# Interleaving two float32 arrays on one Trainium2 core: each stored row of 32 KiB moved as two pieces of 16 KiB

## The chip, the cores and the metric

The kernel runs on one core of one Trainium2 chip. The metric is the device time of one execution in microseconds (us). Lower is better. Besides the times there is one profiled execution, whose page and trace are read below.

## The reference

Two float32 arrays of 32 x 256 x 1024 elements (32 MiB each) are woven into one of 32 x 256 x 2048 (64 MiB): even places hold x, odd places hold y.

```python
result = np.zeros((batch, seq, dim * 2), dtype=np.float32)
result[..., 0::2] = x
result[..., 1::2] = y
```

Nothing is calculated. The kernel reads 67.11 MB, writes 67.11 MB, and between the two puts every element in its place in on-chip memory.

## The kernel before

The arrays are taken as flat memory and cut into n = 8 blocks. One block of x (or y) is 128 partitions x 8192 floats: each partition holds one contiguous row of 32 KiB, 4 MiB in all. One block of the output is twice as long, 128 rows of 64 KiB, and is stored in two halves (h = 0 and 1) of 128 x 32 KiB, 4 MiB each. So a full load moves 128 rows of 32 KiB, and so does a full store.

There are two buffers for x (`xt`), two for y (`yt`) and two for the woven output (`ot`), all 128 x 8192 floats. `xt` and `yt` alternate by block, `ot` by half.

Three engines work, each with its own order of instructions, tied by semaphores alone:

- **SP issues all loads** on its DMA queue, in this order: the first x block as two halves of 2 MiB (L42, L43), then y of block 0 (L53), x and y of block 1 (L50, L53) and so on. From block 2 on, x of block k waits until the second x copy of block k-2 is done, and y of block k until the second y copy of it is done (the semaphore `woven`, which counts copies). So the loads of block k are issued when block k-2 has been woven completely, and by then only the loads of block k-1 can still be under way.
- **VectorE (DVE) weaves.** For each block and half it copies 128 x 4096 floats of x to the even places of `ot[h]` (L67) and as many of y to the odd places (L70): 32 copies in all. The copy at L67 waits until x has landed and until the previous store from the same `ot[h]` has landed (`osem[h]`); L70 waits for y.
- **The ACT sequencer issues all stores** on its own DMA queue, one for each half when its two copies are done (L83). The very first store is cut in two: 8 KiB of every row (L77, 1 MiB, semaphore `qsem`) and the other 24 KiB (L81, 3 MiB).

At the end ACT waits for the last store from `ot[0]` and SP for the last from `ot[1]`. After the body is written, two SP loads (L42, L43) are moved ahead of the opening barrier, so that they start at once.

What sets the order around the change is therefore: the load queue (17 DMAs), the store queue (17 DMAs), both feeding the same 16 DMA engines, and the copies between them.

Of the kernel before, what the change touches and what calls it, by code (L numbers as in the profile page):

```python
# [3 lines left out]


def _interleave(nc, x, y, out):
    P = 128
    W = 8192
    H = W // 2  # L10

    total = 1
    for s in x.shape:
        total *= s
    n = total // (P * W)
    assert n * P * W == total

    def rows(ap, names, k):
        flat = ap.rearrange("b s d -> (b s d)")
        return flat[k * names : (k + 1) * names].rearrange("(p w) -> p w", p=P)  # L20

    fp32 = mybir.dt.float32
    xt = [nc.alloc_sbuf_tensor(f"xt{b}", [P, W], fp32).ap() for b in (0, 1)]
    yt = [nc.alloc_sbuf_tensor(f"yt{b}", [P, W], fp32).ap() for b in (0, 1)]
    ot = [nc.alloc_sbuf_tensor(f"ot{b}", [P, W], fp32).ap() for b in (0, 1)]

    xsem = [nc.alloc_semaphore(f"xsem{b}") for b in (0, 1)]
    hsem = nc.alloc_semaphore("hsem")
    qsem = nc.alloc_semaphore("qsem")
    ysem = [nc.alloc_semaphore(f"ysem{b}") for b in (0, 1)]  # L30
    woven = nc.alloc_semaphore("woven")
    osem = [nc.alloc_semaphore(f"osem{b}") for b in (0, 1)]


    cuts = [0, W // 4, W]
    parts = [slice(a, b) for a, b in zip(cuts, cuts[1:])]

    xs = [rows(x, P * W, k) for k in range(n)]
    ys = [rows(y, P * W, k) for k in range(n)]
    os_ = [rows(out, 2 * P * W, k) for k in range(n)]  # L40

    nc.sync.dma_start(out=xt[0][:, :H], in_=xs[0][:, :H]).then_inc(xsem[0], 16)  # L42
    nc.sync.dma_start(out=xt[0][:, H:], in_=xs[0][:, H:]).then_inc(hsem, 16)  # L43

    for k in range(n):
        b = k % 2
        if k >= 2:
            nc.sync.wait_ge(woven, 4 * (k - 2) + 3)
        if k:
            nc.sync.dma_start(out=xt[b], in_=xs[k]).then_inc(xsem[b], 16)  # L50
        if k >= 2:
            nc.sync.wait_ge(woven, 4 * (k - 2) + 4)
        nc.sync.dma_start(out=yt[b], in_=ys[k]).then_inc(ysem[b], 16)  # L53

    for k in range(n):
        b = k % 2
        for h in (0, 1):
            c = slice(h * H, (h + 1) * H)
            if h == 0:
                nc.vector.wait_ge(xsem[b], 16 * (k // 2 + 1))  # L60
            elif k == 0:
                nc.vector.wait_ge(hsem, 16)
            if k:
                nc.vector.wait_ge(osem[h], 16 * k)
            if (k, h) == (1, 0):
                nc.vector.wait_ge(qsem, 16)
            nc.vector.tensor_copy(out=ot[h][:, 0::2], in_=xt[b][:, c]).then_inc(woven, 1)  # L67
            if h == 0:
                nc.vector.wait_ge(ysem[b], 16 * (k // 2 + 1))
            nc.vector.tensor_copy(out=ot[h][:, 1::2], in_=yt[b][:, c]).then_inc(woven, 1)  # L70

    for k in range(n):
        for h in (0, 1):
            nc.scalar.wait_ge(woven, 4 * k + 2 * h + 2)
            if (k, h) == (0, 0):
                for c in parts[:-1]:
                    nc.scalar.dma_start(  # L77
                        out=os_[k][:, c], in_=ot[h][:, c]
                    ).then_inc(qsem, 16)
                c = parts[-1]  # L80
                nc.scalar.dma_start(out=os_[k][:, c], in_=ot[h][:, c]).then_inc(osem[h], 16)  # L81
                continue
            nc.scalar.dma_start(  # L83
                out=os_[k][:, h * W : (h + 1) * W], in_=ot[h]
            ).then_inc(osem[h], 16)

    nc.scalar.wait_ge(osem[0], 16 * n)
    used = sorted(s.num for s in [*xsem, hsem, qsem, *ysem, woven, osem[0]])
    assert used == list(range(used[0], used[-1] + 1)), used
    nc.scalar.sem_clear(range(used[0], used[-1] + 1))  # L90
    nc.sync.nop(nofuse=True).wait_op(osem[1], 16 * n, "sem-ge").then_inc(
        osem[1], -16 * n
    )


def kernel(tc, x, y, out):
    nc = tc.nc
    tc.close()
    tc.compile()

    _interleave(nc, x, y, out)

    blocks = nc.main_func.blocks
    for engine in (mybir.EngineType.SP, mybir.EngineType.SP):
        opening = blocks[0].instructions
        at, moved = next(
            (b, i)
            for b in blocks[1:]
            for i in b.instructions
            if i.engine == engine and i.opcode == "DMACopy"  # L110
        )
        assert not (moved.sync_info and moved.sync_info.on_wait)
        body = at.instructions
        body.remove(moved)
        gate = next(
            n
            for n, i in enumerate(opening)
            if i.engine == engine and i.opcode == "Drain"
        )
        opening.insert(gate, moved)  # L120
        at.instructions = body
        blocks[0].instructions = opening


# [1 line left out]
_INS = ['x', 'y']  # L126
_OUTS = [((32, 256, 2048), 'float32')]


# [23 lines left out]
```

## Time and profile before

| what | value |
|---|---|
| time, median of 3 runs | 314.11 us (314.11 to 314.13) |
| span of the profiled execution | 312.9 us |
| what the median adds to the span | 1.2 us (314.11 - 312.9) |
| VectorE busy | 72.0 us in 32 copies, 23% of the span |
| DMA | 134.22 MB at a mean of 429 GB/s |
| load queue (q1) | 2448 packets, 67.11 MB |
| store queue (q10) | 2448 packets, 67.11 MB |

The profiled execution's time is known by its span, from its first to its last instruction; the median of the runs is 1.2 us longer, for what lies before and after. A packet is one piece of contiguous memory moved by one of the 16 DMA engines, or the 4-byte semaphore update by which an engine tells that its share of a DMA has landed. The share of a queue is the time that its packets took, as a part of the time of 16 engines over the span. Besides the page, the trace holds a record of each packet: its queue, bytes, start and duration.

The packets can be counted from the code. Every DMA of 128 rows gives each of the 16 engines 8 rows. The load queue carries 17 DMAs of 128 rows, so 17 x 128 = 2176 rows and 17 x 16 = 272 semaphore updates: 2448. The store queue has 17 DMAs too, and the same count.

### The profile page before, as it was taken

The numbers are of one execution on the slowest core, as the hardware profiler recorded it, in microseconds if no ns is written. First come the engines' busy times: TensorE is split into PE (matmuls) and PEld (weight loads), VectorE is DVE, ScalarE is ACT, GpSimd is POOL, SyncE is SP. The second block draws the span as 40 slices with busy tenths as digits, with TensorE's granted clock in tenths as the row PEclk, the third lists the DMA queues.
The fourth block names the chain that finished last, engine by engine and source line by source line (L and its number), as shares of the span: only waits on it lengthen the run. The fifth ranks groups of instructions, "written<-read, shape, count | busy, mean of one in ns | idle before, by whom it ended". The sixth has DMA issues, their size and how long they took to land.

```text
span 312.9 us, 114 instructions
## 1 busy us (share of the span) xinstructions
DVE 72.0 (23%) x32; POOL 0.2 (0%) x4
## 2 busy tenths in 40 slices
DVE  0216000501305023050220503205032050415410
POOL 0000000000000000000000000000000000000000
DMA  8999999999999999999999999999999999999998
GB/s 337 467 402 436 436 402 419 452 457 415 427 444 411 461 402 469 402 469 402 469 402 465 406 440 432 423 448 402 469 402 469 402 469 402 469 402 448 423 423 381
DMA packets 4896, 134.22 MB, mean 429 GB/s; under 512 B 544, under 2 KB 544, under 8 KB 544
## 3 DMA queue, kind: packets, MB, share of 16 engines
q1 hardware_dynamic: 2448, 67.11, 50.1%
q10 hardware_dynamic: 2448, 67.11, 49.7%
HBM read 67.11 MB, written 67.11 MB: 429 GB/s over the span
## 4 chain that ended last, share of the span: by engine, by line
DMA 82%; DVE 12%; issue 0%
DMA out_dram<-ot 76%; DMA yt<-in_y_dram 6%; DVE ot L70 6%; DVE ot L67 6%
## 5 line engine op out<-in xcount | busy, mean ns | idle before, releaser
L67 DVE COPY ot<-xt 128x4096 f32<-128x4096 f32 x16 | 36.7, 2295 | 213.8 <-DMA out_dram<-ot 206.5
L70 DVE COPY ot<-yt 128x4096 f32<-128x4096 f32 x16 | 36.6, 2288 | 12.3 <-DMA yt<-in_y_dram 12.3
L137 POOL MEMSET const-bfloat16-1.0<- 128x1 bf16 x1 | 0.1, 103 | 0.0
L137 POOL MEMSET const-uint8-127<- 128x1 uint8 x1 | 0.1, 102 | 0.0
L137 POOL MEMSET const-float32-0.0<- 128x1 f32 x1 | 0.1, 100 | 0.2 <-issue 0.2
L137 POOL MEMSET const-float32-1.0<- 128x1 f32 x1 | 0.1, 99 | 0.0
## 6 DMA issues: line engine op xcount, KB each, us to landing
out_dram<-ot ACTq DMA_DIRECT2D x15, 4096.0 KB, 34.1
yt<-in_y_dram SPq DMA_DIRECT2D x8, 4096.0 KB, 41.5
xt<-in_x_dram SPq DMA_DIRECT2D x7, 4096.0 KB, 24.3
xt<-in_x_dram SPq DMA_DIRECT2D x2, 2048.0 KB, 9.5
out_dram<-ot ACTq DMA_DIRECT2D x1, 3072.0 KB, 32.8
out_dram<-ot ACTq DMA_DIRECT2D x1, 1024.0 KB, 16.3
```

The lines of the kernel that those rows point to most:

```text
L67: nc.vector.tensor_copy(out=ot[h][:, 0::2], in_=xt[b][:, c]).then_inc(woven, 1)
L70: nc.vector.tensor_copy(out=ot[h][:, 1::2], in_=yt[b][:, c]).then_inc(woven, 1)
L137: nc = _bacc.Bacc("TRN2", target_bir_lowering=False, num_devices=1)
```

## The change

Stores name their rows as two pieces. The access pattern of the store, on the on-chip side and on the memory side, goes from (128 rows x 8192 floats) to (128 rows x 2 pieces x 4096 floats); for the second part of the first store from (128 x 6144) to (128 x 2 x 3072). The bytes, their places and the order of the stores stay. The helper writes the instruction itself, with the same queue as before, so that the two pieces stay separate in the pattern. The first part of the first store (8 KiB rows) and all loads are as before. No wait, buffer or copy changes, and no instruction is added on any engine: ACT issues 17 DMAs as before, 16 of them with the new pattern.

```diff
+QUEUES = {
+    mybir.EngineType.SP: "qSPDynamicHW",
+    mybir.EngineType.Activation: "qActDynamicHW",
+}
+
+def _piece_copy(engine, out, in_, s):
+
+    ins, outs = (
+        engine.lower_ap_dma(ap.rearrange("p (s w) -> p s w", s=s)) for ap in (in_, out)
+    )
+    return engine.add_instruction(
+        mybir.InstDMACopy(
+            mode="Copy",
+            name=engine.bass.get_next_instruction_name(),
+            engine=engine.engine,
+            ins=ins,
+            outs=outs,
+            queue=QUEUES[engine.engine],
+        )
+    )
...
                 c = parts[-1]
-                nc.scalar.dma_start(out=os_[k][:, c], in_=ot[h][:, c]).then_inc(osem[h], 16)
+                _piece_copy(nc.scalar, os_[k][:, c], ot[h][:, c], 2).then_inc(osem[h], 16)
                 continue
-            nc.scalar.dma_start(
-                out=os_[k][:, h * W : (h + 1) * W], in_=ot[h]
+            _piece_copy(
+                nc.scalar, os_[k][:, h * W : (h + 1) * W], ot[h], 2
             ).then_inc(osem[h], 16)
```

## The prediction

> **What bounds the kernel now.** I read the page's busy lines first, then its DMA queues, then the chain of work that ended last, then the packet records.
>
> ```profile
> DVE 72.0 (23%) x32; POOL 0.2 (0%) x4
> ...
> DMA  8999999999999999999999999999999999999998
> ...
> q1 hardware_dynamic: 2448, 67.11, 50.1%
> q10 hardware_dynamic: 2448, 67.11, 49.7%
> ```
>
> VectorE works 23% of the span. The 16 DMA engines are full from the second slice to the last but one: the two queues' packets take 50.1 + 49.7 = 99.8% of all engine time. So the DMA engines are the bound, in every stage; a chain that names stores only says which transfer a copy happened to wait for:
>
> ```profile
> 76.83 2.29 DVE ot L67
> 79.12 2.21 DVE ot L70
> 81.34 0.02 issue
> 81.36 34.17 DMA out_dram<-ot
> 115.53 0.02 issue
> 115.55 2.29 DVE ot L67
> 117.85 2.21 DVE ot L70
> 120.06 0.02 issue
> 120.08 34.17 DMA out_dram<-ot
> ```
>
> The columns are start, length and what. The steady round is 115.55 - 76.83 = 38.72 us, in which one block (8 MiB in, 8 MiB out) moves. A store lands 34.17 us after its issue, though its own share of an engine is only 8 rows: it waits behind the store before it and shares the engines with the loads. Bandwidth in stretches says the same:
>
> ```profile
> 13.00:24.00 11.00, 2.09 (x1) 0.00 (x0) 1.00 1.00 432
> ...
> 100.00:260.00 160.00, 36.78 (x17) 0.00 (x0) 1.00 1.00 433
> ```
>
> (The last columns are the DMA share and GB/s.) Loads alone reach 432, loads and stores mixed 433. Nothing is lost by mixing.
>
> **What one packet costs.** The packet records do not name the engine, but a record starts where its predecessor on the same engine ended, so they fall into 16 chains. I take the step from one start to the next. In the steady part 32 KiB rows step by 1209.5 ns (2249 of them, mean), loads or stores alike. The 16 KiB rows of the first two loads step by 607.0 ns. The first store's 8 KiB and 24 KiB rows lie alternately with 32 KiB load rows, in cycles of 1515.4 and 2117.7 ns; less 1209.5 that is 305.9 and 908.2 ns. All four lie on one line: 602.4 ns for 16 KiB plus 4.7 ns a packet. So cutting a 32 KiB row in two costs 2 x 607.0 - 1209.5 = 4.5 ns, or 4.7 by the line; the store rows alone (8 and 24 KiB) give 305.9 - 602.3 / 2 = 4.7.
>
> **Who is served.** The same chains show the order: with both queues waiting, an engine takes one row of one queue, then one of the other, whatever their sizes. Around 100 us one engine starts q10 at 99.244, q1 at 100.453, q10 at 101.663, each 32 KiB; around 35 us it takes an 8 KiB store row (306 ns), a 32 KiB load row (1209), and so on. The small store then got a fifth of the engine. This matters more than the cost of the packet.
>
> **The change part by part.**
>
> *Added packets.* Sixteen stores of 128 rows become 256 pieces each: 16 x 128 = 2048 packets more, 128 on each engine. At 4.7 ns that is 128 x 4.7 = 0.60 us (0.58 by the 4.5). Since the engines have no idle time, nothing hides it. The bytes and the 272 semaphore updates stay.
>
> The Trainium skill, page DMA: Bandwidth & Descriptors, section Why small descriptors are slow (HBM only), gives a fixed overhead of about 3 cycles a packet, and its Specifications a fabric of 850 MHz; an estimate from these is 128 x 3.5 ns = 0.45 us, and the time would be 314.56. The rows here say 4.7 ns, and rows decide.
>
> *Shares.* While loads wait too, an engine now alternates 1209.5 ns of load and 607 ns of store. Stores fall from a half of the engine to a third. Loads of one block (16 rows on each engine) need 16 x (1209.5 + 607) = 29.1 us instead of 38.7. Then SP can issue nothing until the next block is woven, and stores run alone for 16 x 607 = 9.7 us. Together 38.8 us: the same round. I followed both queues, the copies and the waits row by row by these rules; for the kernel before it gives 311.6 us to the last landing, where the chains end at 312.2 to 312.5. For the change no engine is ever without a packet. The closest places: the first 24 KiB store lands near 67 us instead of 57, so the first copy of block 1 starts 10 us later, its store is issued near 72, but the store ahead ends only near 79; and at the end the last store is issued some 4.5 us before the one ahead of it has ended, in both kernels (here 298.1 against 302.6). If that cover were gone, a hole of a copy pair and the start of a store would stand open, 4.5 us and about 1 us (SP's first load: issued at 0.00, first packet at 0.99).
>
> *Issues.* An ACT issue takes 0.34 us (L83); a pattern with twice the pieces could take longer, which I bound by nothing and twice that, 0.34 us. Behind it on ACT stands only the next store's wait, about 14 us off in the steady part, so I take zero.
>
> *Load queue falling idle.* This is new. In the trace before, the load queue never runs dry until 277 us. Now it does once a round, and wakes for blocks 3 to 7: five times. Before shows one such wake beside a busy queue, the first store's: between 25 and 33 us each engine's rows run late by 0.35 to 0.62 us, median 0.46. Loads starting on idle engines lost 0.73 (median, first 5 us). The other neighbour is the ending of the loads at 277 us: rows step 1209 before and after, zero. So one wake costs 0 to 0.73 us, five of them 0 to 3.6. I take zero, nearest to this row: a store row (SBUF to memory) is already in the pipe at each wake, as after 277, while at 25 us the first write of all entered. Memory reads need time to start, but a row that is asked for early hides it: the first store's rows ran some 3.4 us after they could (issue done at 24.62, first row near 28.7, against 0.6 us on an idle engine).
>
> *Sum.* Span 312.86 + 0.60 = 313.46; with the 1.25 us around it 314.71, against 314.11. That is +0.19%, and about 0.2% (0.63 us, to 314.74) is what a measurement of this kernel can tell from no change. The forecast stands on the edge of it.
>
> **Rivals.**
>
> *B, slower: each wake of the load queue costs.* Place: the first load row after stores ran alone, five times. Price: at 0.46 us each 2.3, so 317.0; at 0.73, 318.4; at 0.1, 315.2. It decides from about 0.01 us each, since the packets already stand at the bound. For it: the one wake seen, late on all 16 engines. Against: three later changes of pattern (57 us, 24 to 32 KiB; 277 us; the 16 to 32 KiB loads at 11.5) cost nothing that can be seen.
>
> The same page, section Queues, rings and completion order, has an engine drain a packet of some 9 to 17 descriptors from one ring before it turns; then a whole DMA's share would be one turn, loads and stores would keep their halves, the load queue would not fall idle, B would be out, and the time would be that of the sum. The trace disagrees: it turns after each row.
>
> *C, no change: the pieces are joined again* on the way to the engines (they are contiguous on both sides). Then 314.11. Against it: the built pattern keeps 2 x 4096, and rows of 16 KiB do exist on the load side.
>
> *D, faster: the losses at the start shrink.* Behind 31 us the chains lose only 0.08 us (39 to 43.5 us, median) and nothing after. If the change gave back all of that 0.08 and all of the first store's 0.46, it would still add 0.60 - 0.54 = 0.06 us: 314.17 at best. A gain of over 0.2% would need faster rows, and all four sizes lie on one line.
>
> **How the numbers follow.** Forecast 0.55 (314.6 to 314.9 by 4.5 to 5.1 ns a packet and a possible 0.1 at the start); of it I put 0.32 within the bound and 0.23 above. B 0.30. C 0.07. Something that opens a hole in the store queue 0.05, slower. D or any other gain 0.03. So faster 0.03, same 0.32 + 0.07 = 0.39, slower 0.23 + 0.30 + 0.05 = 0.58. The likeliest single case is still the plain sum, 314.71. Range: from C, 314.1, to 317.4, which takes in B up to 0.53 us a wake, and leaves out about a quarter of B, D, and half of the holes: some 0.13 to 0.15.
>
> **What would show it.** Store queue: 2448 + 2048 = 4496 packets at the same 67.11 MB; 2448 would be C. Loads land sooner: x about 19 us after issue instead of the 24.3 of the page's DMA issues, y about 31 instead of 41.5; stores stay near 34. Unchanged landings with 4496 packets would mean that the shares are not by row. The longest wait of L67 grows from 29.0 to about 38.7 us. The steady round is 38.8 us; 39.3 would be B at 0.46. DMA stays at 9s throughout; an 8 in the middle would be a hole. I am wrong if the time is below 314.1, or if a round stays at 38.8 and the time still rises.

## The result, and the profile after

| | before | after |
|---|---|---|
| time, median | 314.14 us (314.11 to 314.40, 6 runs) | 315.21 us (315.16 to 316.75, 6 runs) |
| span of the profiled execution | 312.9 us | 313.9 us |

The change is 1.07 us slower by the medians: a ratio of 1.004, 95% interval 1.0026 to 1.0053. That lies inside the range and on the side that held most of the chance, but half a microsecond above the sum of 314.71, and above the 314.6 to 314.9 that were given to the sum. One of the six runs took 316.75; the six of the kernel before lie within 0.3 us.

The page of the changed kernel, DMA slices and queues (packets, MB, share of 16 engines):

```profile
DMA  8999999999999999999999999999999999999998
...
DMA packets 6944, 134.22 MB, mean 428 GB/s; under 512 B 544, under 2 KB 544, under 8 KB 544
...
q1 hardware_dynamic: 2448, 67.11, 50.0%
q10 hardware_dynamic: 4496, 67.11, 49.9%
```

The store queue has 4496 packets, as counted, so the pieces stay apart. The engines are as full as before, 99.9%, and no slice shows a hole. What takes longer is therefore in the packets themselves.

The DMA issues of the page before, then of the same page after (KB each, median us from issue to landing):

```profile
out_dram<-ot ACTq DMA_DIRECT2D x15, 4096.0 KB, 34.1
yt<-in_y_dram SPq DMA_DIRECT2D x8, 4096.0 KB, 41.5
xt<-in_x_dram SPq DMA_DIRECT2D x7, 4096.0 KB, 24.3
```

```profile
out_dram<-ot ACTq DMA_DIRECT2D x15, 4096.0 KB, 34.2
yt<-in_y_dram SPq DMA_DIRECT2D x8, 4096.0 KB, 31.7
xt<-in_x_dram SPq DMA_DIRECT2D x7, 4096.0 KB, 18.8
```

Loads land after 18.8 and 31.7 us (about 19 and 31 were forecast; before 24.3 and 41.5), stores as late as before. The engines do alternate packet by packet, and loads have two thirds of the time while both wait. From the changed kernel's chain of waits (start, length, what), one round, and the starts of the later ones:

```profile
85.20 0.02 issue
85.22 34.39 DMA out_dram<-ot
119.61 0.02 issue
119.64 2.29 DVE ot L90
121.93 2.21 DVE ot L93
124.14 0.02 issue
124.17 34.40 DMA out_dram<-ot
...
163.10 0.02 issue
...
201.90 0.02 issue
...
240.71 0.02 issue
...
279.50 0.02 issue
```

This round is 124.14 - 85.20 = 38.94 us where 38.80 was forecast; the later ones are 38.96, 38.80, 38.81 and 38.79. The first two rounds are longer by 0.15 us each, the others are as forecast. The longest wait of the first copy grew from 29.0 to 37.6 us (38.7 forecast), by the views of the waits before and after:

```profile
DVE ot L67 <- DMA out_dram<-ot: 206.5, 14, 29.0
```

```profile
DVE ot L90 <- DMA out_dram<-ot: 207.4, 14, 37.6
```

**The ledger by packet records.** For each of the 16 chains I take every step from one packet's start to the next, less what the line gives (602.4 ns for 16 KiB, plus 4.7 ns). What is left is lateness. Mean of 16 engines, in us, and the start of the last semaphore packet of the middle and of the slowest engine:

| kernel | 0 to 50 us | after 50 us | middle engine ends | slowest ends |
|---|---|---|---|---|
| before | 1.18 | 0.00 | 312.34 | 312.47 |
| after | 1.35 | 0.12 | 313.15 | 313.48 |

The slowest engine ends 1.00 us later. Of that 0.60 are packets, 0.17 the first 50 us, and 0.12 late rows in the rounds (23 rows late by over 20 ns, all of them 32 KiB load rows, near 97, 136 and 174 us). The rest, about 0.1, is the balance of two terms: engines end farther apart (0.33 us from the middle one to the slowest, 0.13 before), and their first packets start 0.07 us earlier in the mean. Each of the three is small, and the experiments ask which of them belongs to the change.

### The profile page after: what moved, and what is told of

It reads as the page before. It is cut to its first block, busy times and chain, and to the rows that moved or that the text cites. A ratio compares the mean times of both kernels' runs of the same rounds, so it can differ in the third digit from the quotient of the medians.

```text
span 313.9 us, 114 instructions
## 1 busy us (share of the span) xinstructions
DVE 72.0 (23%) x32; POOL 0.2 (0%) x4
## 3 DMA queue, kind: packets, MB, share of 16 engines
q1 hardware_dynamic: 2448, 67.11, 50.0%
q10 hardware_dynamic: 4496, 67.11, 49.9%
## 4 chain that ended last, share of the span: by engine, by line
DMA 79%; DVE 12%; another core or an unknown queue 3%; issue 0%; ACTq 0%; DVEq 0%
DMA out_dram<-ot 73%; DVE ot L93 6%; DMA yt<-in_y_dram 6%; DVE ot L90 6%; ACTq L100 0%; DVEq L89 0%
## 5 line engine op out<-in xcount | busy, mean ns | idle before, releaser
L93 DVE COPY ot<-yt 128x4096 f32<-128x4096 f32 x16 | 36.6, 2290 | 12.3 <-DMA yt<-in_y_dram 12.3
## 6 DMA issues: line engine op xcount, KB each, us to landing
yt<-in_y_dram SPq DMA_DIRECT2D x8, 4096.0 KB, 31.7
xt<-in_x_dram SPq DMA_DIRECT2D x7, 4096.0 KB, 18.8
out_dram<-ot ACTq DMA_DIRECT2D x1, 3072.0 KB, 41.5
```

## Experiments

The theory is the sum: 4.7 ns for every packet more, nothing else. Against it stood that each wake of the load queue costs (rival B), that cut stores make the stall at the start longer, and that the helper's instruction itself costs. The kernel before was timed beside each set: 314.23 us (26 runs) beside the first four kernels, 314.22 (9) beside the next four, 314.33 (9) beside the last two.

### one_piece: the helper without the cut

```diff
-                _piece_copy(nc.scalar, os_[k][:, c], ot[h][:, c], 2).then_inc(osem[h], 16)
+                _piece_copy(nc.scalar, os_[k][:, c], ot[h][:, c], 1).then_inc(osem[h], 16)
...
-                nc.scalar, os_[k][:, h * W : (h + 1) * W], ot[h], 2
+                nc.scalar, os_[k][:, h * W : (h + 1) * W], ot[h], 1
```

> The helper writes the stores, but each row stays one piece (128 x 1 x 8192, first store 128 x 1 x 6144): the change without its cut. Theory of the sum (4.7 ns for every packet more, plus a stall when the first stores join): 2448 packets on the store queue, time as before, 314.1 to 314.4; the engines run late by about 0.48 us between 25 and 33.5 us, as before. Rival, the helper itself costs (its instruction differs): 315.2 with 2448 packets.

Measured 314.30 us, ratio 1.0002 (0.9993 to 1.0011), 2448 packets. The helper costs nothing, though an ACT issue takes 0.48 us with it (0.34 before, 0.61 with two pieces): the issue is hidden. Lateness from 0 to 50 us is 1.17, after that 0.00.

### first_block_whole: 14 of 16 stores cut

```diff
+                _piece_copy(nc.scalar, os_[k][:, c], ot[h][:, c], 1).then_inc(osem[h], 16)
...
+                nc.scalar, os_[k][:, h * W : (h + 1) * W], ot[h], 2 if k else 1
```

> The three stores of block 0 keep whole rows, the other 14 are cut in two: 14 x 8 = 112 packets more on each engine. Theory that the part beyond the sum (1.07 us measured, 0.60 of it packets) is the longer issue of cut stores at the start: 0.53 us of packets and no more, 314.65 to 314.8, with 0.48 us late at 25 to 33.5 us. Rival, the stall at the start varies from run to run and has nothing to do with the cut: as the whole change less 0.08, about 315.1. Rival, each wake of the load queue costs: five wakes remain, the excess stays, about 315.1, and rows run late at the five wakes.

Measured 315.03 us, ratio 1.0038 (1.0023 to 1.0052); three of the nine runs took 315.51 to 317.14. The stall between 25 and 33.5 us is 0.50, 0.48 before, and still the time is 0.80 above, not 0.53. So here the start is not where the excess comes from. The load queue falls idle four times in this kernel, not the five that were expected: with whole stores in block 0 it does not run dry before block 3. Three engines have late rows (0.10, 0.19 and 0.38 us in the rounds); the engine with 0.38 is the one that ends last, at 313.31 against 312.96 for the middle one.

### first_block_only: two stores cut, at the start

```diff
+                nc.scalar, os_[k][:, h * W : (h + 1) * W], ot[h], 1 if k else 2
```

> Only block 0 is cut (the 24 KiB part of the first store and the second half): 16 packets more on each engine, 0.08 us. Theory that cut stores at the start make the stall longer: 0.08 + about 0.25, 314.4 to 314.5, with about 0.73 us late at 25 to 33.5 us. Rival, the stall does not hang on the cut: 314.2, and 0.48 late or the same scatter as in the other runs. By the shares the 24 KiB store lands near 66 us, and the loads then fall idle once, before block 3; a cost of that wake would show there alone.

Measured 314.33 us, ratio 1.0008 (0.9999 to 1.0016): 0.10 above the kernel before, as the 0.08 of its packets. The stall is 0.58, between the two forecasts. The load queue falls idle once, for 15.2 us from 72 us on, and wakes beside whole stores: no engine has a late row there or later, so in this profile a wake as such costs nothing. Two of the 11 runs took 314.97 and 315.13, as none of the 26 of the kernel before did; they have no profile, and what they lost is not known.

### as_change: the change once more

> The whole change again, on this chip: 315.1 to 315.3 by the first result. If the stall at the start is a matter of the run, its size between 25 and 33.5 us differs from the 0.73 us seen first; if it hangs on the cut it is again 0.7 or so.

Measured 315.73 us where 315.1 to 315.3 was expected, in two groups: 315.11, 315.12, 315.16 and 316.31, 316.45, 316.90. The kernel before stayed within 0.3 us beside it. The profile is of the 316.31 run, one of the longer group. Its span

```profile
core 0: 315.0 us, clock 1.000
```

is 1.1 us longer than in the first profile, though its stall between 25 and 33.5 us is shorter (0.52 for 0.73), so that stall varies from run to run. After 50 us the engines are late by 0.36 us in the mean, but two of them by 1.6 and 1.1. These two lose 0.48 and 0.55 us at 242.6 us, in the store piece just ahead of the load queue's wake, and more in load rows soon after. The kernel ends with them, at 314.58, 1.4 us after the middle engine.

### both_halved: equal shares again

```diff
-            nc.sync.dma_start(out=xt[b], in_=xs[k]).then_inc(xsem[b], 16)
+            _piece_copy(nc.sync, xt[b], xs[k], 2).then_inc(xsem[b], 16)
...
-        nc.sync.dma_start(out=yt[b], in_=ys[k]).then_inc(ysem[b], 16)
+        _piece_copy(nc.sync, yt[b], ys[k], 2).then_inc(ysem[b], 16)
```

> Stores and the full loads are both cut in two: 128 + 15 x 8 = 248 packets more on each engine, 1.17 us. The queues share the engines by halves again, so the load queue never falls idle. Theory of the sum: 1.17 us and a stall at the start of the same size as in the change (up to 0.3 more than before), 315.3 to 315.6, y landing about 52 us after issue in the steady part, x about 35, the first 24 KiB store near 51 us. Rival, the wakes of the load queue are what the change costs beyond the packets: none here, 315.25 and no stall anywhere.

Measured 315.46 us, 1.24 above; 1.17 were packets. Nearly twice the packets of the change cost only 0.25 us more than it (315.21). The load queue never falls idle, x and y land after 33.4 and 50.7 us (35 and 52 expected), and after 50 us no engine is late (0.00).

### loads_halved: the shares turned round

Loads as in both_halved, stores as in one_piece.

> Only the full loads are cut, stores are whole: 120 packets more on each engine, 0.56 us, fewer than in the change. If packets alone counted: 314.7 to 315.0. If the queues are served row by row (the shares), loads now get a third while stores wait, the store queue falls idle once a round, and the last load lands so late (near 293 us) that the copies of the last block stand with the engines empty: one hole of some 3.9 us before the last two stores, 318.5 to 318.9.

Measured 326.59 us, ratio 1.0387 (1.0368 to 1.0405): a hole of the kind that was forecast, in its place, but the cost 12.4 us and not 4.4. The page shows it in slices 37 and 38, and the windows show it in their last two columns (DMA share, GB/s):

```profile
DMA  8999999999999999999999999999999999994599
```

```profile
290.00:294.00 4.00, 0.00 (x0) 0.00 (x0) 1.00 0.93 401
294.00:298.00 4.00, 0.00 (x0) 0.00 (x0) 1.00 0.48 205
298.00:302.00 4.00, 0.57 (x1) 0.00 (x0) 1.00 0.05 20
302.00:306.00 4.00, 4.00 (x3) 0.00 (x0) 1.00 0.30 131
```

Between 298 and 302 us the engines are nearly empty, while VectorE waits for y of the last block. The packet records tell why the hole is so large: the 16 engines start their last load row between 291.0 and 300.5 us, and the load has landed only with the last of them. Sixteen engines that were alike in the kernel before (their last load row starts between 274.7 and 275.0) have drifted 9.5 us apart. Rows have been late by 2.8 us in the mean of the engines after 45 us, the hole apart; by 7.4 us on the engine that ends its loads last, and by 1.6 on those that lost least.

### four_pieces and eight_pieces: smaller pieces in the stores alone

> Stores in four pieces of 8 KiB (6 KiB in the first store): 3 x 128 = 384 packets more on each engine, 1.81 us at 4.7 ns. Theory of the sum: 315.9 plus a stall at the start (0 to 0.6 more than before, as the issue takes longer still), 315.9 to 316.5; x lands about 15 us after issue, y about 25. Rival, the wakes cost: the load queue is idle longer, and rows run late at each of five wakes.

> Stores in eight pieces of 4 KiB (3 KiB in the first store): 7 x 128 = 896 packets more on each engine, 4.2 us at 4.7 ns. Theory of the sum: 318.3 to 319.1 with the stall at the start. If small pieces cost more than the line of the four sizes says, the step of a 4 KiB packet is above 155 ns and the time above 319.1. If the issue of a store (0.34 us whole, 0.61 in two pieces) grows by 0.27 us a piece it takes 2.2 us, still covered by the store ahead of it.

The number in the helper's last argument is 4, then 8. Measured 317.22 us (3.00 above, 1.80 of it packets) and 321.69 (7.47 above, 4.2 of it packets), beyond the 316.5 and 319.1 that the sum allowed at most. The steps are on the line: 306 ns for 8 KiB, 155 for 4 KiB (median; by the line 155.3). The excess is for the most part lateness: late rows of 0.80 and 2.60 us in the mean of 16 engines. With four pieces it lies where the load queue wakes (87, 126, 165, 205, 244 us) and where it has ended its round (110, 150, 189, 228, 267). The median issue did not grow with the pieces: ACT needs 0.61 us with 2, 4 and 8. One of the 16 issues with eight pieces took 7.50 us, at 28.6 us.

### both_eight and four_and_two: small pieces, or unequal shares?

Both start from both_halved; the last argument of the helper is 8 for stores and loads, or 4 for stores and 2 for loads.

> Stores and full loads are both cut in eight pieces of 4 KiB: 896 + 15 x 56 = 1736 packets more on each engine, 8.2 us at 4.7 ns; the shares are equal, and the load queue never falls idle. Theory that what the cut stores cost beyond their packets comes from unequal shares (rows run late, and the engines drift apart): none here after 50 us, 322.3 to 322.8 in all, all engines end within 0.4 us of each other. Rival, small packets themselves run late beside another queue: with eight pieces in the stores alone each engine lost 2.6 us after 45 us; here twice as many, 325 to 328.

> Stores in four pieces (8 KiB), full loads in two (16 KiB): 384 + 120 = 504 packets more on each engine, 2.37 us. The shares are 1 to 2 as in the change, and the load queue falls idle every round. Theory that unequal shares with a queue that falls idle make rows late: 2.4 us and 0.3 to 1.5 beyond it, 316.9 to 318.1, with late rows in the rounds after 50 us and engines that end up to 1 us apart. Rival, the lateness belongs to 32 KiB load rows beside smaller packets, which do not occur here: 316.5 to 316.7 with no late rows.

With eight pieces on both sides: 322.61 us, 8.28 above, where 8.2 are packets. Not one row is late after 45 us, and the slowest engine ends 0.24 us after the middle one. The page of this kernel:

```profile
q1 hardware_dynamic: 15888, 67.11, 51.0%
q10 hardware_dynamic: 16784, 67.11, 50.7%
```

With four and two: 317.66 us, 3.33 above, where 2.37 are packets; 0.80 us of lateness in the mean, in 16 KiB load rows and 8 KiB store pieces alike. So small packets are not late in themselves, and 32 KiB load rows are not needed for it.

All kernels but loads_halved, by what was added and what was left over (time less the kernel before beside it, less 4.7 ns a packet; the sum of all rows late by over 20 ns after 45 us, mean of 16 engines):

| kernel | shares, load queue | above before, us | packets, us | left over | late rows |
|---|---|---|---|---|---|
| one_piece | equal, busy | 0.07 | 0 | 0.07 | 0.00 |
| first_block_only | unequal at the start, one wake | 0.10 | 0.08 | 0.02 | 0.00 |
| both_halved | equal, busy | 1.24 | 1.17 | 0.07 | 0.00 |
| both_eight | equal, busy | 8.28 | 8.16 | 0.12 | 0.00 |
| first_block_whole | unequal, four wakes | 0.80 | 0.53 | 0.27 | 0.04 |
| the change, first result | unequal, five wakes | 1.07 | 0.60 | 0.47 | 0.12 |
| the change, again | unequal, five wakes | 1.50 | 0.60 | 0.90 | 0.36 |
| four_and_two | unequal, five wakes | 3.33 | 2.37 | 0.96 | 0.80 |
| four_pieces | unequal, five wakes | 3.00 | 1.80 | 1.20 | 0.80 |
| eight_pieces | unequal, five wakes | 7.47 | 4.21 | 3.26 | 2.60 |

With equal shares the sum holds to 0.12 us from no packet added to 1736 on each engine. What is left over comes with a load queue that falls idle and comes back, round after round, beside cut stores.

But the late rows do not sit at the wakes, as long as the pieces are large. In the first profile of the change none does: the late load rows start 8.5 to 12.3 us after the first load row of their round, and nearly all of them (21 of 23) within 2 us of the semaphore packet with which their engine ends its share of a store. At the wakes themselves (from 2 us before the start of an engine's first load row to 1.3 us after it, all wakes together, mean of 16 engines) the late rows sum to:

| kernel | store pieces | late at the wakes, us |
|---|---|---|
| the change, first result | 16 KiB | 0.00 |
| the change, again | 16 KiB | 0.08 |
| four_and_two | 8 KiB | 0.23 |
| four_pieces | 8 KiB | 0.21 |
| eight_pieces | 4 KiB | 1.69 |

So a wake costs more the smaller the store pieces beside it are. That would fit a piece in the pipe that covers the wake while it lasts; no run tests this reason.

## Why the prediction was right or wrong

- **The number.** The time lies in the stated range, but not in the 314.6 to 314.9 of the forecast that was worked out. What put it inside is the room that was given to rival B, and B's mechanism is not the one that the first profile shows. To that extent the hit is luck.
- **The bound and the packet.** Right. DMA engines are full in both kernels, and 4.7 ns a packet holds down to 4 KiB pieces, where the nearest rows ended at 8 KiB. The 0.60 us were the largest single part of the 1.07.
- **The shares.** Right: one packet of each queue in turn. x and y landings, the late first store, the unchanged landing of stores, the length of the round and the idle load queue came out as worked out row by row. The Trainium skill (DMA: Bandwidth & Descriptors, section Queues, rings and completion order) has an engine drain 9 to 17 descriptors from one ring before it turns. The packet records here show one row to a turn, and the landings (18.8 us for x, where it was 24.3) follow from it. loads_halved, which turned the shares round, gave the hole that one row to a turn asks for.
- **The load queue falling idle.** I took zero between 0 and 0.73 us a wake. At the wakes of the first profile zero is what was found, and in the second one 0.08 us in the mean of 16 engines: there a loss of the size of B's price (0.48 and 0.55 us, against 0.46) struck 2 engines of 16 at one of five wakes. My reason for zero, that a store row in the pipe covers the wake, thus held for most engines, with pieces of 16 KiB. What failed is that I looked for a cost at the wake alone. Load rows ran late some 10 us after it, beside the end of a store, for which the sum had no term: 0.12 us in the mean of 16 engines in the first profile, and 0.28 of the 0.36 in the second lie away from the wakes. Rival B was right about the sign, and wrong about the place (the first load row) and about taking 0.46 us for every engine and wake.
- **Averages.** The sum was made for an average engine, but a DMA lands with its slowest one. The distance from the middle engine's end to the slowest's is 0.13 us before (0.20 to 0.24 in the other kernels without late rows), 0.33 in the first profile of the change, 1.42 in the second. In the same way the first two rounds of the first profile grew by 0.15 us each, more than the mean engine lost in all. This term was not in the sum at all.
- **The sign of being wrong.** I named a round that stays at 38.8 us while the time still rises. Three of the five rounds did stay there, and the time rose by 0.47 us more than its packets; some 0.3 of that are the two longer rounds.
- **The start.** I let the stall at the first store stand unchanged. In the change's first profile the first 50 us were later by 0.17 us; but over all profiles this lateness goes from 1.06 (eight_pieces) to 1.37 (both_eight) without order by pieces. By that it is scatter from run to run; one profile of most kernels is too little to show that no part of it is the change.
- **Issues.** The issue grew from 0.34 to 0.61 us, inside the bound. That it cost nothing is shown for 0.48 (one_piece, 314.30); both_halved with 0.61 leaves 0.07 us over its packets, no more than one_piece.
- **The bound of 0.2%.** The sum stood at +0.19% and the result is +0.34% (1.07 / 314.14): the 0.47 us that the sum left out decided the side.

Open stays what makes a row late, and why beside the end of a store. Unequal shares alone do not (first_block_only, and the change itself between 45 and 75 us, where no row is late), and a wake beside whole rows did not in the one profile that has it. No kernel kept unequal shares through all rounds without the queue falling idle, so the two were not tried apart there. Nor is it shown why one run of the same kernel loses 0.12 us and another 0.36.

## What to carry to other kernels

When DMA engines are the bound, count packets: each cost 4.7 ns here, which nothing hid, and cutting a row buys nothing unless another term falls. The two queues shared an engine by packets and not by bytes, so that the size of rows acted as a priority: check which queue then falls idle and which transfer becomes late, as loads_halved lost 12 us where the change lost one. Work such a sum for the slowest engine, for a landing waits for it.

## What the runs showed that was not expected

- Engines that ran alike under equal shares drifted apart under unequal ones: up to 9.5 us in loads_halved by the last load, though every DMA gives each engine the same number of rows.
- The median issue of a store went with the pattern's dimensions, not with the number of pieces: 0.34 us for 128 x 8192, 0.48 for 128 x 1 x 8192, 0.61 for two, four and eight pieces. But in both_eight the median y load took 12.9 us to issue (0.60 in both_halved), with earlier loads still queued, and one store of eight_pieces took 7.5 (min/median/max in ns):

```profile
L18 SPq DMA_DIRECT2D yt<-in_y_dram x8: 602/12875/17484, 1.9 to 234.2; - x8
```

```profile
L18 ACTq DMA_DIRECT2D out_dram<-ot x16: 607/608/7501, 24.6 to 304.4; - x16
```

What these issues waited for is not shown. In both_eight the wait was covered, as the sum held to 0.12 us.
- Runs of one kernel scatter where stores are cut in two and loads are whole: 315.11 to 316.90 in as_change and 314.86 to 317.14 in first_block_whole, where both_halved stayed within 0.2 us and both_eight within 0.4.
